# A hybrid decoder layer on one core: the retention's rotary step is moved out of the values' group

## Chip, cores and metric

The kernel runs on one core of one Trainium2 chip. The metric is the device time of one execution in microseconds (us). The profile shows five engines of that core: PE (matmuls; PEld loads its weights), DVE (vector), ACT (scalar), POOL (GpSimd) and SP, whose queue issues nearly all DMAs.

## What is computed

One decoder layer on 1024 tokens of width 2048, in fp32. A conditioned RMSNorm gives h; one projection `h @ w_in` gives 8192 columns, which are q, k, v, z of eight stick-breaking heads and q, k, v, z of eight retention heads, each of 128 columns. The part that the change touches is the retention's rotary step and the loop behind it:

```python
def rotary(t):
    ...
    t1, t2 = tf[..., :half], tf[..., half:]
    return jnp.concatenate([t1 * cos - t2 * sin, t1 * sin + t2 * cos], axis=-1)
...
qr = rotary(split_heads(q_r, RET_HEADS))
kr = rotary(split_heads(k_r, RET_HEADS)) * (HEAD_DIM ** -0.5)
vr = split_heads(v_r, RET_HEADS).astype(jnp.float32)
ob = head_group_norm(chunkwise_retention(qr, kr, vr), ret_norm_gain[layer])
ob = ob * jax.nn.silu(z_r.astype(jnp.float32))

y = jnp.concatenate([oa, ob], axis=-1).astype(x.dtype) @ w_out[layer]
x = x + (gate[:, None, :] * y).astype(x.dtype)
```

## The kernel before

**Matmuls.** Every fp32 operand is cut into a high part (ACT, line 173) and a low part (DVE, line 175), and each product is three matmuls (`mm3`, lines 186 to 188) of 128x512. The projection and the output product are each done as seven products of half-size blocks (a Strassen scheme). The retention's queries come first, in a stage of their own (tile `first`), and are kept in DRAM unrotated (`rqraw`). Then come seven **groups** of 1024 columns. The first four hold the columns of the stick-breaking heads, two heads each (indices 0 to 3 of the list `groups`), the fifth the retention's keys, the sixth its values (`ACROSS`, computed transposed, by `run_across`), and the seventh its z (`LAST`).

A group has seven **products**, named by the block of h that they use, in the order T4, B11, T2, T1, B22, B21, T3. A product has eight **entries** (four column blocks, two halves of the sum). An entry is 12 matmuls and two **steps**: `tick()` is the program's clock. So a product has 16 steps and a group 112. The weights of an entry are cut three entries ahead (`LOOK`); in the values' group entries go in pairs of four steps. The finished outputs of a group come out in its last three products: half of the first head of each pair after B22's product, the other half after B21's, both halves of the second head after T3's (function `evac`, where `final` takes a finished tile).

**What runs beside it.** Other work is written as generators that are advanced once a step, or as functions due so many steps later (`later`). PE's order is written by hand through these steps. The stick-breaking attention of the heads whose columns a group made runs in the following group: two heads each in the second to fifth group, with a tail in the first product of the next group. A vector-matrix product for the gate (`gate_steps`, tile `gr`) and sums of the output weights (`sum_steps`, tile `s`) are spread over the groups.

**The DMA queue.** SP issues the DMAs in the program's order, and a DMA that has to wait for a buffer, for its data or for an earlier write holds up all behind it. For each product the factors of h come back from DRAM, 16 loads of 256 KB (`fac`, lines 279 and 281), issued 15 to 20 steps before use. Per group there are 32 raw weight loads (lines 264 and 266). All tiles of 128x512 come from one pool of 92 slots.

**The rotary step before.** The keys' group writes its 16 finished tiles (eight heads, two halves of the sequence) to DRAM (`pr_rk`). `turn_in` starts in the values' group, as soon as the last stick-breaking head is nearly done. Every three steps it takes one tile of 128x512, key and query in turn: it loads the tile (line 1393), loads it again with its halves of 64 partitions exchanged (`sw`, lines 1395 and 1396), nine steps later makes three DVE operations (lines 1401, 1402 and 1406 for a query, whose bias is added on the way, 1404 to 1406 for a key) and two steps after that writes the result to DRAM (line 1410). So a tile costs four DMAs and three DVE operations, and there are 32 of them.

**The retention.** `ret_heads` starts six entries before the last group. Each head takes 16 steps (four gaps of `RT_GAP`): it loads keys, queries and values (lines 1432 and 1436) and a mask (`dm`, line 1455), transposes the keys on PE (line 1472, tile `ktp`), makes states (line 1480, tile `up`), scores (line 1498), masked scores on DVE (line 1503, tile `pT`) and values. The eighth head begins at the third step of the output product.

Of the kernel before, what the change touches and what calls it, by code (L numbers as in the profile page):

```python
# [17 lines left out]
P = 128  # L18
# [14 lines left out]
RT_GAP = 4  # L33
# [63 lines left out]
def layer_kernel(ctx, tc, x, c, w_ada, b_ada, norm_gain, w_in, sb_q_gain, sb_k_gain, ret_norm_gain, w_out,  # L97
# [18 lines left out]
    proj = {f"{n}{h}": dr.tile([P, S], F32, name=f"pr_{n}{h}") for n in ("q", "k", "z", "v", "rk")  # L116
# [274 lines left out]
    def evac(gi, prod, q, o):  # L391
# [595 lines left out]
    def bias_steps():  # L987
# [37 lines left out]
        nc.scalar.activation(qb[64:128, 1, 0:NZ], qb[0:64, 0, 0:NZ], AF.Copy)  # L1025

# [353 lines left out]
    def turn_in():  # L1380

        while prog.get(NH - 1, 0) < 12:
            yield 1
        for i, n in enumerate(("cos", "sin")):
            for hf in range(2):
                tables[n, hf] = t = get(f"{n}_{hf}", "att")
                nc.sync.dma_start(t, rot[i][:, halves(hf)])
        yield 2

        def one(n, h, hf):  # L1390
            src = proj[f"rk{h}"] if n == "k" else rqraw[h]
            t = get(f"r{n}_{h}_{hf}", "att")
            nc.sync.dma_start(t, src[:, halves(hf)])
            sw = get(f"sw_{n}{h}_{hf}", "att")
            nc.sync.dma_start(sw[0:64, :], src[64:128, halves(hf)])
            nc.sync.dma_start(sw[64:128, :], src[0:64, halves(hf)])
            cos, sin = tables["cos", hf], tables["sin", hf]

            def rotate():
                if n == "q":  # L1400
                    nc.vector.scalar_tensor_tensor(sw, sw, qb[:, 1, h:h + 1], sin, op0=ALU.add, op1=ALU.mult)
                    nc.vector.scalar_tensor_tensor(t, t, qb[:, 0, h:h + 1], cos, op0=ALU.add, op1=ALU.mult)
                else:
                    nc.vector.tensor_tensor(sw, sw, sin, op=ALU.mult)
                    nc.vector.tensor_tensor(t, t, cos, op=ALU.mult)
                nc.vector.tensor_tensor(t, t, sw, op=ALU.add)
                put(sw)

            def back():
                nc.sync.dma_start(turned_in[n, h][:, halves(hf)], t)  # L1410
                put(t)
                turns[0] += 1
            later(9, rotate)
            later(11, back)

        for h in range(NH):
            for n in "kq":
                for hf in range(2):
                    one(n, h, hf)
                    yield 3  # L1420
        yield 12
        put(*tables.values())

    turns = [0]

    def ret_prepare(h):
# [12 lines left out]
        def values_in(n):  # L1439
            later(n, lambda: load_v(0))  # L1440
            later(n + 1, lambda: load_v(1))
# [9 lines left out]
    def ret_attention(h, r, gap):  # L1451
# [125 lines left out]
        yield gap  # L1577
# [4 lines left out]
        yield gap  # L1582
# [3 lines left out]
        yield gap  # L1586
# [4 lines left out]
        yield gap  # L1591
# [3 lines left out]
    def ret_heads():  # L1595
        nxt, values_in = ret_prepare(0)
        while phase[0] < 6:
            yield 1
        values_in(3)
        yield 2  # L1600
        for h in range(NH):
            r = nxt
            for i, wait in enumerate(ret_attention(h, r, RT_GAP)):
# [388 lines left out]
```

## Time and profile before

| | us |
|---|---|
| median of three runs (lowest 1941.51, highest 1945.44) | 1941.53 |
| the profiled execution, by its own time | 1946.04 |
| its span in the trace | 1944.0 |
| PE busy (share of the span) | 1882.3 (97%) |
| DVE busy | 1340.7 (69%) |
| ACT busy | 816.6 (42%) |
| POOL busy | 82.1 (4%) |
| bytes moved by DMA | 557.81 MB, mean 287 GB/s |

The page gives the busy time of each engine, then the span in 40 slices of 48.6 us: a digit is the busy share in tenths, and PEclk is the clock that PE was granted. The view by windows gives the same for chosen stretches, with the DMA engines' busy share and the bytes per second. The view of waits says who waited for whom. Matmuls are pipelined, so the mean duration of one (about 390 ns) is longer than the distance between two (about 227 ns).

### The profile page before, as it was taken

The numbers are of one execution on the slowest core, as the hardware profiler recorded it, in microseconds if no ns is written. First come the engines' busy times: TensorE is split into PE (matmuls) and PEld (weight loads), VectorE is DVE, ScalarE is ACT, GpSimd is POOL, SyncE is SP. The second block draws the span as 40 slices with busy tenths as digits, with TensorE's granted clock in tenths as the row PEclk, the third lists the DMA queues.
The fourth block names the chain that finished last, engine by engine and source line by source line (L and its number), as shares of the span: only waits on it lengthen the run. The fifth ranks groups of instructions, "written<-read, shape, count | busy, mean of one in ns | idle before, by whom it ended". The sixth has DMA issues, their size and how long they took to land.

```text
span 1944.0 us, 28991 instructions
## 1 busy us (share of the span) xinstructions
PE 1882.3 (97%) x9501; PEld 1546.4 (80%) x9501; DVE 1340.7 (69%) x2601; ACT 816.6 (42%) x1543; POOL 82.1 (4%) x278
## 2 busy tenths in 40 slices
PE   8999999999999999999999999977779999999998
PEld 6777788888888888888888888755668888888887
DVE  3568775666769686867686868864664547596769
ACT  3647752234544454445444543211124446543221
POOL 0000000000010001000000000000010100000000
PEclk9999999999999999999999999988889999999999
DMA  9979999998797989797978988999976664995594
GB/s 318 364 240 314 316 356 371 364 325 293 243 311 248 316 264 332 252 319 249 351 255 286 292 319 282 297 323 322 346 266 217 225 219 147 334 370 188 169 312 164
DMA packets 417522, 557.81 MB, mean 287 GB/s; under 512 B 35166, under 2 KB 203480, under 8 KB 417372
## 3 DMA queue, kind: packets, MB, share of 16 engines
q1 hardware_dynamic: 416508, 555.57, 85.9%
q8 instruction: 75, 1.23, 0.3%
q14 instruction: 75, 0.61, 0.1%
q10 hardware_dynamic: 864, 0.40, 0.1%
HBM read 461.42 MB, written 94.41 MB: 286 GB/s over the span
## 4 chain that ended last, share of the span: by engine, by line
PE 85%; DMA 9%; DVE 3%; issue 1%; SPq 1%; ACT 0%; ACTq 0%; DVEq 0%
PE pj L186 17%; PE pj L187 17%; PE pj L188 17%; PE y L188 4%; PE y L186 4%; PE y L187 4%; PE first L186 3%; PE first L188 2%; PE first L187 2%; PE accp L607 1%; DMA sw_k<-pr_rk 1%; DMA A<-in_w_in_dram 1%; PE tp_B L1286 1%; DMA rq<-rqraw 1%; PE oT L186 1%
## 5 line engine op out<-in xcount | busy, mean ns | idle before, releaser
L173 ACT ACTIVATE wh<-A 128x512 fp32r<-128x512 f32 x392 | 247.2, 632 | 469.7 <-PE pj L187 319.3
L175 DVE TENSOR_TENSOR wl<-A,wh 128x512 fp32r<-128x512 f32 x392 | 269.4, 689 | 210.5 <-ACT wh L173 200.2
L395 ACT ACTIVATE c<-pj 128x512 f32<-128x512 f32 x112 | 66.4, 600 | 135.2 <-PE pj L188 118.5
L302 DVE TENSOR_TENSOR A<-A,A 128x512 f32<-128x512 f32 x160 | 109.8, 694 | 1.7
L398 DVE TENSOR_TENSOR c<-pj,c 128x512 f32<-128x512 f32 x112 | 74.5, 687 | 42.4 <-PE pj L188 41.8
L1250 ACT ACTIVATE om<-zp,y 128x128 f32<-128x128 f32 (+2 forms) x96 | 55.8, 581 | 107.4 <-PE zp L188 67.2
L186 PE MATMUL first<-h_hi,wh_first 128*128 128x512 f32 x224 | 95.1, 424 | 0.6 <-ACT h_hi L636 0.6
L1266 DVE TENSOR_TENSOR_SCAN om<-om 128x128 f32<-128x128 f32 (+2 forms) x96 | 93.5, 974 | 1.2
L187 PE MATMUL first<-h_lo,wh_first 128*128 128x512 f32 x224 | 88.7, 396 | 0.2 <-DVE h_lo L638 0.2
L188 PE MATMUL first<-h_hi,wl_first 128*128 128x512 f32 x224 | 88.7, 396 | 0.0
L186 PE MATMUL pj<-T4h,wh 128*128 128x512 f32 x192 | 78.7, 410 | 5.6 <-issue 3.8
L186 PE MATMUL pj<-T1h,wh 128*128 128x512 f32 x200 | 81.5, 408 | 0.0
L186 PE MATMUL pj<-B22h,wh 128*128 128x512 f32 x200 | 80.1, 401 | 0.0
L186 PE MATMUL pj<-B21h,wh 128*128 128x512 f32 x200 | 79.6, 398 | 0.0
L186 PE MATMUL pj<-B11h,wh 128*128 128x512 f32 x200 | 78.8, 394 | 0.0
L188 PE MATMUL pj<-T1h,wl 128*128 128x512 f32 x200 | 78.3, 391 | 0.0
L188 PE MATMUL pj<-B22h,wl 128*128 128x512 f32 x200 | 78.2, 391 | 0.0
L187 PE MATMUL pj<-T1l,wh 128*128 128x512 f32 x200 | 78.1, 391 | 0.0
L187 PE MATMUL pj<-B21l,wh 128*128 128x512 f32 x200 | 78.0, 390 | 0.0
L187 PE MATMUL pj<-B22l,wh 128*128 128x512 f32 x200 | 78.0, 390 | 0.0
L188 PE MATMUL pj<-B21h,wl 128*128 128x512 f32 x200 | 78.0, 390 | 0.0
L187 PE MATMUL pj<-B11l,wh 128*128 128x512 f32 x200 | 78.0, 390 | 0.0
(450 smaller groups left out, 5125.2 us busy)
## 6 DMA issues: line engine op xcount, KB each, us to landing
A<-in_w_in_dram SPq DMA_DIRECT2D x228, 256.0 KB, 5.6
ada<-in_w_ada_dram SPq DMA_DIRECT2D x120, 256.0 KB, 5.5
wB<-in_w_out_dram SPq DMA_DIRECT2D x112, 256.0 KB, 5.6
gr<-in_w_ada_dram SPq DMA_DIRECT2D x64, 256.0 KB, 5.8
T2h<-fac_T SPq DMA_DIRECT2D x56, 256.0 KB, 5.5
T2l<-fac_T SPq DMA_DIRECT2D x56, 256.0 KB, 5.5
T1h<-fac_T SPq DMA_DIRECT2D x56, 256.0 KB, 5.4
T1l<-fac_T SPq DMA_DIRECT2D x56, 256.0 KB, 5.3
```

The lines of the kernel that those rows point to most:

```text
L173: nc.scalar.activation(hi[:, 0:n], src[:, 0:n], AF.Copy)
L175: nc.vector.tensor_tensor(lo[:, 0:n], src[:, 0:n], hi[:, 0:n].bitcast(F32), op=ALU.subtract)
L186: nc.tensor.matmul(o, a_hi, b_hi, start=first, stop=False, skip_group_check=on)
L187: nc.tensor.matmul(o, a_hi, b_lo, start=False, stop=False, skip_group_check=on)
L188: nc.tensor.matmul(o, a_lo, b_hi, start=False, stop=last, skip_group_check=on)
L302: nc.vector.tensor_tensor(r[o], r[a], r[b], op=ALU.add if n == 1 else ALU.subtract)
L395: nc.scalar.activation(t, o, AF.Copy)
L398: nc.vector.tensor_tensor(dst[q, cc], o, dst[q, cc], op=ALU.add)
L607: nc.tensor.matmul(ap_[32 * g:32 * g + 32, :], silu_z[:, j, :], ada[cc, j // 2][:, (j % 2) * 256:(j % 2) * 256 + 256], start=j < 4, stop=j ...
L1250: nc.scalar.activation(om[:, :n], zp[:, :n], AF.Sigmoid, scale=y[:, 16 + i:17 + i])
L1266: nc.vector.tensor_tensor_scan(rev, rev, rev, init, op0=ALU.mult, op1=ALU.bypass)
L1286: nc.tensor.transpose(banks_[j // 2][:, c0:c0 + P], be[:, j * P:(j + 1) * P], ident)
```

## The change

The values' group and the keys' group change places: values are the fifth group, keys the sixth. `turn_in` is gone. The 16 query tiles are rotated in three lots, six tiles in the third group and five each in the fourth and fifth, one tile every four steps from step 10 of the group on; the three operations stand seven steps behind the loads, and the write one step behind those. The cos and sin tables are loaded anew for each lot, and once more for the keys. A key tile isn't written to DRAM and loaded again: one step after it is finished two DMAs copy its halves of 64 partitions crosswise into a second SBUF tile, seven steps later the three operations follow, and one step after these the write. The retention's heads go in the order 0, 2, 4, 6, 1, 3, 5, 7; the first starts when its two key tiles have been written, at step 106 of the keys' group (before: at step 3 of the last group), and a head takes 17 steps in place of 16, so that the last begins two steps earlier than before. In all, SP issues 20 DMAs fewer (2166 for 2186); PE and DVE have the same operations as before.

```diff
-RT_GAP = 4
+RT_GAPS = (4, 4, 4, 5)
+QUERY_GAP = 4
+QUERIES = {2: 6, 3: 5, 4: 5}
...
-    groups.append([(5 * GW + a * P, proj[f"rk{a}"], proj[f"rk{a + 1}"]) for a in range(0, NH, 2)])
 
     ACROSS = len(groups)
     groups.append([(6 * GW, None, None)] * 4)
+    KEYS = len(groups)
+    groups.append([(5 * GW + a * P, a, a + 1) for a in range(0, NH, 2)])
     groups.append([(7 * GW + a * P, a, a + 1) for a in range(0, NH, 2)])
...
+            if gi == KEYS:
+                sw = get(f"sw_k{to}_{hf}", "att")
+
+                def swap():
+                    nc.sync.dma_start(sw[0:64, :], t[64:128, :])
+                    nc.sync.dma_start(sw[64:128, :], t[0:64, :])
+                later(1, swap)
+                later(8, lambda: rotate("k", to, hf, t, sw))
+                return
...
-    def turn_in():
-
-        while prog.get(NH - 1, 0) < 12:
-            yield 1
...
+    def rotate(n, h, hf, t, sw):
+
+        cos, sin = tables["cos", hf], tables["sin", hf]
+        if n == "q":
+            nc.vector.scalar_tensor_tensor(sw, sw, qb[:, 1, h:h + 1], sin, op0=ALU.add, op1=ALU.mult)
+            nc.vector.scalar_tensor_tensor(t, t, qb[:, 0, h:h + 1], cos, op0=ALU.add, op1=ALU.mult)
+        else:
+            nc.vector.tensor_tensor(sw, sw, sin, op=ALU.mult)
+            nc.vector.tensor_tensor(t, t, cos, op=ALU.mult)
+        nc.vector.tensor_tensor(t, t, sw, op=ALU.add)
+        put(sw)
+
+        def back():
+            nc.sync.dma_start(turned_in[n, h][:, halves(hf)], t)
+            put(t)
+            turned.add((n, h, hf))
+        later(1, back)
...
+    def turn_queries(n):
+
+        assert bias_done
+        yield 8
+        load_tables()
         yield 2
...
+        for _ in range(n):
+            h, hf = queries.popleft()
+            t = get(f"rq_{h}_{hf}", "att")
+            nc.sync.dma_start(t, rqraw[h][:, halves(hf)])
+            sw = get(f"sw_q{h}_{hf}", "att")
+            nc.sync.dma_start(sw[0:64, :], rqraw[h][64:128, halves(hf)])
+            nc.sync.dma_start(sw[64:128, :], rqraw[h][0:64, halves(hf)])
+            later(7, lambda h=h, hf=hf, t=t, sw=sw: rotate("q", h, hf, t, sw))
+            yield QUERY_GAP
+        yield 7
         put(*tables.values())
...
         load("k", 0)
         later(1, lambda: load("q", 0))
+        later(3, lambda: load_v(0))
         later(4, lambda: load("k", 1))
         later(5, lambda: load("q", 1))
-        if h:
-            values_in(3)
-        return r, values_in
...
     def ret_heads():
-        nxt, values_in = ret_prepare(0)
-        while phase[0] < 6:
+        heads = (0, 2, 4, 6, 1, 3, 5, 7)
+        while not {("k", 0, 0), ("k", 0, 1)} <= turned:
             yield 1
-        values_in(3)
-        yield 2
-        for h in range(NH):
+        nxt = ret_prepare(0)
+        yield 7
+        for i, h in enumerate(heads):
...
-            if gi == 5:
-                start(turn_in(), 1)
+            if gi in QUERIES:
+                run_apart(turn_queries(QUERIES[gi]))
+            if gi == KEYS:
+                run_apart(for_keys())
+                start(ret_heads(), 1)
```

**The queries' lots, on SP.** This is SP's order in the second product of the third group, around the small write `krow` of the stick-breaking keys' scales and its load back `kb`. `s` are loads of output weights, `concat` is the output of a finished head. Before:

```order
L1089 DMA s_1_0_7182<-in_w_out_dram 128x512
L1089 DMA s_1_0_7183<-in_w_out_dram 128x512
L1345 DMA concat_78<-zr_1_6474 128x512
L1174 DMA krow_164<-yr_7161 8x128
L1182 DMA kb_0_7219<-krow_164 128x512
L1182 DMA kb_1_7221<-krow_164 128x512
L1185 DMA q_0_7223<-pr_q_104 128x512
L1185 DMA q_1_7224<-pr_q_104 128x512
```

And now, with a tile's three loads (`rq`, `sw_q` twice) and the writes of earlier tiles (`rot_q`):

```order
L1102 DMA s_1_0_7201<-in_w_out_dram 128x512
L1102 DMA s_1_0_7202<-in_w_out_dram 128x512
L1358 DMA concat_78<-zr_1_6466 128x512
L1187 DMA krow_156<-yr_7180 8x128
L1430 DMA rq_1_7229<-rqraw_95 128x512
L1432 DMA sw_q_1_7231<-rqraw_95 64x512
L1433 DMA sw_q_1_7231<-rqraw_95 64x512
L1408 DMA rot_q_146<-rq_1_7083 128x512
L1195 DMA kb_0_7247<-krow_156 128x512
L1195 DMA kb_1_7249<-krow_156 128x512
L1198 DMA q_0_7251<-pr_q_104 128x512
L1198 DMA q_1_7252<-pr_q_104 128x512
```

Two loads of a query tile and a write have come between `krow` and `kb`, and another four rows ahead of them.

**The end of the rotated keys, on SP.** This is where the first retention head's keys are loaded (`rk_0<-rot_k`, first head, first half). `A` are raw weights of the next group, `rv` values. Before, at the end of the values' group:

```order
L1396 DMA sw_q_1_15222<-rqraw_101 64x512
L266 DMA A_6_1_1_15235<-in_w_in_dram 128x4x128
L1432 DMA rk_0_15237<-rot_k_146 128x512
L1410 DMA rot_k_153<-rk_0_15069 128x512
L1432 DMA rq_0_15246<-rot_q_154 128x512
L1039 DMA gr_6_15267<-in_w_ada_dram 128x2x256
L279 DMA T4h_6_15271<-fac_T_6_216 128x512
L281 DMA T4l_6_15273<-fac_T_6_216 128x512
L279 DMA T4h_7_15275<-fac_T_7_217 128x512
```

And now, at steps 97 to 103 of the keys' group, where `rot_k_138` is the first head's:

```order
L416 DMA sw_k_0_15073<-c_5_3_14268 64x512
L417 DMA sw_k_0_15073<-c_5_3_14268 64x512
L269 DMA A_6_3_0_15099<-in_w_in_dram 128x4x128
L1408 DMA rot_k_138<-c_5_0_14206 128x512
L269 DMA A_6_0_1_15122<-in_w_in_dram 128x4x128
L1452 DMA rk_0_15124<-rot_k_138 128x512
L1452 DMA rq_0_15135<-rot_q_146 128x512
L1408 DMA rot_k_140<-c_5_1_14224 128x512
L269 DMA A_6_1_1_15149<-in_w_in_dram 128x4x128
L1456 DMA rv_0_15160<-rvt_0_134 128x4x128
L1452 DMA rk_1_15173<-rot_k_138 128x512
```

Before, the keys that are loaded had been written long ago (a write `rot_k` beside them is another head's); now the load stands two rows behind the write of the same tile.

**The same stretch on DVE,** at the beginning of the last group: from the cut `wl` of one entry's weights to that of the next, `ga` being the gate's sums and `A` sums of raw weights. Before:

```order
L175 TENSOR_TENSOR wl_4_3_0_15376<-A_6_3_0_14686,wh_4_3_0_15374 128x512
L1048 SCALAR_TENSOR_TENSOR ga_13330<-gr_6_15267,silu_c,ga_13330 128x256 x2
L302 TENSOR_TENSOR A_6_0_0_14601<-A_6_0_0_14601,A_6_0_0_15093 128x512
L302 TENSOR_TENSOR A_6_0_0_15093<-A_6_0_0_14844,A_6_0_0_15093 128x512
L175 TENSOR_TENSOR wl_4_0_1_15411<-A_6_0_1_14728,wh_4_0_1_15409 128x512
```

And now, with both halves of a key tile (`c` and `sw_k`, lines 1402 to 1404) in between:

```order
L177 TENSOR_TENSOR wl_4_3_0_15376<-A_6_3_0_14672,wh_4_3_0_15374 128x512
L1061 SCALAR_TENSOR_TENSOR ga_13476<-gr_6_15215,silu_c,ga_13476 128x256 x2
L305 TENSOR_TENSOR A_6_0_0_14581<-A_6_0_0_14581,A_6_0_0_15012 128x512
L1402 TENSOR_TENSOR sw_k_1_15231<-sw_k_1_15231,sin_14595 128x512
L1403 TENSOR_TENSOR c_5_0_14568<-c_5_0_14568,cos_14591 128x512
L1404 TENSOR_TENSOR c_5_0_14568<-c_5_0_14568,sw_k_1_15231 128x512
L1402 TENSOR_TENSOR sw_k_0_15233<-sw_k_0_15233,sin_14593 128x512
L1403 TENSOR_TENSOR c_5_0_13997<-c_5_0_13997,cos_14589 128x512
L1404 TENSOR_TENSOR c_5_0_13997<-c_5_0_13997,sw_k_0_15233 128x512
L305 TENSOR_TENSOR A_6_0_0_15012<-A_6_0_0_14789,A_6_0_0_15012 128x512
L177 TENSOR_TENSOR wl_4_0_1_15422<-A_6_0_1_14691,wh_4_0_1_15420 128x512
```

Six operations of a key tile pair have come between two cuts; three more such pairs follow, one between each of the next cuts.

More of the change, by code (lines that the diff above doesn't have):

```diff
@@ L115, in layer_kernel @@
     rqraw = [dr.tile([P, S], F32, name=f"rqraw{h}") for h in range(NH)]
-    proj = {f"{n}{h}": dr.tile([P, S], F32, name=f"pr_{n}{h}") for n in ("q", "k", "z", "v", "rk")
+    proj = {f"{n}{h}": dr.tile([P, S], F32, name=f"pr_{n}{h}") for n in ("q", "k", "z", "v")
             for h in range(NH)}
@@ L1387, in turn_in, with for_keys @@
                 nc.sync.dma_start(t, rot[i][:, halves(hf)])
-        yield 2
[L1390 to L1414, printed above, removed]
-        for h in range(NH):
[L1417 to L1421, printed above, removed]
-        put(*tables.values())
-    turns = [0]
+    queries = deque((h, hf) for h in range(NH) for hf in range(2))
+    def turn_queries(n):
+        assert bias_done
+        yield 8
+        load_tables()
+        yield 2
+        for _ in range(n):
[8 more added lines that the diff above has]
+        yield 7
+        put(*tables.values())
+    def for_keys():
+        yield 60
+        load_tables()
+        while len(turned) < 4 * NH:
+            yield 1
+        put(*tables.values())
     def ret_prepare(h):
@@ L1576, in ret_attention @@
         scores(0)
[L1577 removed]
+        yield RT_GAPS[0]
         turn_k(1)
@@ L1792, in layer_kernel @@
             cut_right(3 - left_over, 0)
-        if gi == ACROSS and j + 6 < len(entries) and entries[j + 6][0] != ACROSS and entries[j + 5][0] == ACROSS:
-            start(ret_heads(), 1)
         if gi != ACROSS:
```

26 lines of the change are left out of this document (14 added, 12 removed).

## The prediction

> **What bounds the kernel now.** I read the page first: which engine is busy, and where it is not.
>
> ```profile
> span 1944.0 us, 28991 instructions
> ...
> PE 1882.3 (97%) x9501; PEld 1546.4 (80%) x9501; DVE 1340.7 (69%) x2601; ACT 816.6 (42%) x1543; POOL 82.1 (4%) x278
> ...
> PE   8999999999999999999999999977779999999998
> ...
> PEclk9999999999999999999999999988889999999999
> ```
>
> PE bounds the kernel. Its only weak place is slices 27 to 30 (1264 to 1458 us), where it is seven to eight tenths busy and its clock drops too. Next comes the view by windows, cut where PE changes from one product to the next. Columns: stretch, its length, busy us of each engine, then PEclk, DMA share and GB/s.
>
> ```profile
> 229.00:403.00 174.00, 174.00 (x770) 144.06 (x769) 112.48 (x176) 64.65 (x110) 0.00 (x0) 1.00 1.04 357
> 622.00:646.00 24.00, 24.00 (x113) 19.59 (x112) 18.32 (x34) 8.60 (x16) 0.00 (x0) 1.00 0.58 192
> 646.00:672.00 26.00, 26.00 (x126) 21.50 (x125) 14.53 (x26) 12.03 (x25) 3.04 (x14) 1.00 1.03 350
> 820.40:842.50 22.10, 22.00 (x99) 17.91 (x98) 16.67 (x34) 8.30 (x15) 0.00 (x0) 1.00 0.81 276
> 1182.70:1197.00 14.30, 14.17 (x78) 12.01 (x77) 14.00 (x25) 4.04 (x8) 0.00 (x0) 1.00 0.93 326
> 1211.00:1255.30 44.30, 44.28 (x194) 36.00 (x193) 38.75 (x64) 13.02 (x22) 0.00 (x0) 1.00 0.96 299
> 1255.30:1392.50 137.20, 104.08 (x386) 79.50 (x384) 77.97 (x126) 24.90 (x42) 0.00 (x0) 0.87 1.04 326
> 1392.50:1439.80 47.30, 33.93 (x149) 28.43 (x150) 28.27 (x56) 7.85 (x13) 2.55 (x2) 0.79 0.98 330
> 1439.80:1622.80 183.00, 183.00 (x1037) 158.70 (x1037) 100.33 (x307) 88.46 (x166) 15.53 (x12) 1.00 0.65 215
> ```
>
> 1211 to 1255 are two products of the values' group, B11 and T2, with no PE stall: 22.15 us each, 1.38 us a step. The next four take 137.2 us where 4 x 22.15 = 88.6 would do: 48.6 lost. The last group's first product takes 47.3; its other six take 30.5 each with a retention head in every 16 steps (8.4 us a head), so with 13 steps of a head it should take 28.9: 18.4 lost. Together 67.0 us are at stake. Who ends the waits there:
>
> ```profile
> DVE sw_q L1401 <- DMA sw_q<-rqraw: 31.7, 12, 5.7
> PEld pj L187 <- DVE wl L175: 26.7, 11, 7.2
> DVE sw_k L1404 <- DMA sw_k<-pr_rk: 22.5, 8, 6.6
> PE pj L187 <- DVE wl L175: 21.6, 9, 6.8
> PE up L1480 <- DMA rv<-rvt: 11.6, 1, 11.6
> DVE pT L1503 <- DMA dm<-in_ret_mask_dram: 13.6, 1, 13.6
> ```
>
> PE waits for cut weights, DVE cuts them in order behind a rotation, and the rotation waits for its exchanged halves. And the transfers are late because there are too many (DMA issues of 1255.3 to 1392.5):
>
> ```profile
> DMA packets 33835, 44.68 MB, mean 326 GB/s; under 512 B 3049, under 2 KB 15648, under 8 KB 33828
> ...
> rq<-rqraw SPq DMA_DIRECT2D x11, 256.0 KB, 5.8
> sw_q<-rqraw SPq DMA_DIRECT2D x22, 128.0 KB, 6.0
> rot_k<-rk SPq DMA_DIRECT2D x11, 256.0 KB, 6.2
> rk<-pr_rk SPq DMA_DIRECT2D x10, 256.0 KB, 6.1
> sw_k<-pr_rk SPq DMA_DIRECT2D x20, 128.0 KB, 5.4
> ...
> rk<-rot_k SPq DMA_DIRECT2D x1, 256.0 KB, 6.0
> ```
>
> The view lists 190 issues in 137.2 us: 1.39 a us, with the DMA engines at 1.04 (the window's row). Between 229 and 403 they are at 1.04 too; there nearly all transfers have 256 KB (0.262 MB), and 357 GB/s are 1.36 a us. So with 42 half-size transfers among the 190 the bytes fall, the number stays, and a half lands no sooner than a whole tile (5.4 and 6.0 us against 5.8 and 6.1). I take 1.39 DMAs a us as the limit, whatever their size. The stretch held 21 rotated tiles (11 `rq`, 10 `rk`), so one cost PE 48.6 / 21 = 2.3 us.
>
> **The change part by part.** *Rotation leaves the values' group.* A product of 16 steps asks there for 16 factors, some 5 raw tiles, 2 gate tiles and 16/3 x 4 = 21 transfers of the rotation: 44, or 32 us of DMA in 22 us of PE. Without the rotation it is 23, or 17 us, and PE is late for nothing. The last group's first product lost its time to `rv`, loaded right behind the writes of the values, and to `dm`, late in the same queue; the values are now written a whole group earlier. So both losses go, 1946.0 - 67.0 = 1879.0, and what is late next is below.
>
> *Values' group fifth, beside stick-breaking heads.* Its weights are cut only four steps ahead, not six. At 1182.7 this mixture stands already, since the last heads' tail runs in the values' first product: DVE is busy 14.00 of 14.30 us and PE 14.17, without a wait of note. Cost 0; if a fuller mixture differs, it shows in C.
>
> *The queries' lots.* In the third group's second product SP's count rises from 28 to 44, in 24.0 us, in which 33 go: 11 are left, 8 us behind. What covers that? Before, B11 and T2 of the values' group asked for 82 (by SP's order) in 44.3 us, in which 62 go: 20 left, 15 us behind, and PE stood nowhere. The operations now stand seven steps behind the loads, not nine, which takes 2 x 1.38 off: 12 us of cover for 8. The next product (26.0 us, 31 asked, 36 go) pays back. SP itself waits for DVE at each `rot_q`, with the factors queued behind; those are issued 16 steps (22 us) ahead of use and take some 6, so that they can stand the 8 too. On DVE a tile is three operations at their distance in the timeline:
>
> ```profile
> 1270.29 0.68 DVE L1404 TENSOR_TENSOR sw_k<-sw_k,sin 128x512 f32<-128x512 f32 x1
> 1270.89 0.68 DVE L1405 TENSOR_TENSOR rk<-rk,cos 128x512 f32<-128x512 f32 x1
> 1271.61 0.69 DVE L1406 TENSOR_TENSOR rk<-rk,sw_k 128x512 f32<-128x512 f32 x1
> 1272.21 0.69 DVE L175 TENSOR_TENSOR wl<-A,wh 128x512 fp32r<-128x512 f32 x1
> ```
>
> That is 1.9 us, and four tiles are 8 us a product. In the third group 18.32 + 8 is 2.3 over the 24.0, in the fourth 16.67 + 8 is 2.6 over the 22.1; what is queued behind a rotation are the cuts of weights, and three entries of them stand ready (6 x 1.38 = 8.3 us). Cost 0; if the cover fails, 16 x 2.3 = 37. Below zero it can't be: nothing is taken away there, and PE has no wait to lose.
>
> *Keys rotated as they come.* Up to step 80 little is asked (9 to 19 DMAs in 8 steps). In the last 32 steps it is 91: 49 factors, raw and gate tiles, 22 exchanges, 8 writes of rotated keys, 12 loads for the first two retention heads. That takes 65 us, where PE needs 44 and some 3 for the first head's beginning: up to 18 behind. Ahead of the write of the first head's key (step 99) are 46 of them, in 19 steps: 33 us for 26, 7 behind. The load of that key waits for the write. The nearest wait of this kind is
>
> ```profile
> SPq L1182 <- DMA krow<-yr: 5.1, 4, 1.9
> ```
>
> a load behind a write of 4 KB, which SP waited out each time. Here a whole tile's write takes 6.2 (`rot_k`) and the load 6.0 (`rk<-rot_k`): 7 + 12.2 = 19.2 us behind step 99. PE wants the tile for `ktp` at step 106, 9.7 us behind step 99. So PE waits 9.5, or 2.5 if SP is level; I take 7, nearer to the upper end, because the writes of the other heads' keys, each waiting for DVE, keep SP from running ahead before it.
>
> `dm` stands 21 rows behind that load: 15 us, and 5.5 to land, so 14.5 us after the key has landed. DVE's `pT`, due one step after `ktp`, waits for it, as it did for 13.6 before. Behind `pT` stand, up to the cut for step 16 of the last group, 50 operations of 128x512 (24 of them rotations) at 0.60 us, 6 of the gate, 7 of the states and 8 of the statistics:
>
> ```profile
> L1048 DVE SCALAR_TENSOR_TENSOR ga<-gr,silu_c,ga 128x256 f32<-128x256 f32 x17 | 8.2, 482 | 0.3
> L1490 DVE SCALAR_TENSOR_TENSOR state<-state,up 128x128 f32<-128x128 f32 x6 | 1.7, 286 | 0.2
> ```
>
> 30 + 2.9 + 2.0 and some 2 for the statistics: 37 us. PE has from step 106 to there 6 x 1.38, the 3 of the head's beginning and 16 x 1.9: 41.7 us. So 14.5 + 37 - 41.7 = 10 late. Bounds: 4 if `dm` leaves sooner, 14 if the exchanges are late as well. A wait of PE also costs clock:
>
> ```profile
> 1298.88 0.80 PE L187 MATMUL pj<-wl,B22h 128*128 128x512 f32 x1 [6.78 <-DVE wl L175]
> 1299.48 0.63 PE L188 MATMUL pj<-wh,B22l 128*128 128x512 f32 x1
> 1299.90 0.63 PE L186 MATMUL pj<-wh,B22h 128*128 128x512 f32 x1
> ```
>
> matmuls 0.42 us apart, not 0.227: 1 to 2 us each time, 3 in all. Sum for this end 7 + 10 + 3 = 20.
>
> How soon an exchange inside SBUF lands, no row shows. The nearest are the halves from DRAM (5.4 and 6.0), far below them the small write (1.9 at most). I take 5.5, by the halves, which have the same shape; at 1.9 the 22 exchanges hold no place in the queue for long, and SP is level there. The Trainium skill (SBUF — State Buffer, "The DMA setup-cost knee") has a fixed cost of about 2 us and bytes over 436 GB/s: an estimate of 2.3 us for a half, and the end would cost about 11, not 20. The rows of the halves are more than twice that, so the trace doesn't agree so far.
>
> *Heads of 17 steps, nine steps earlier.* Same matmuls; the last head starts two steps sooner. 0.
>
> **Sum:** 1879.0 + 20 = 1899 on the profiled execution. That execution lay 4.5 us above the median of 1941.53, beside the slowest of the three runs (1945.44); I take off 4: 1895.
>
> **The rivals.** *A, the forecast:* 1895, own range 1882 to 1904 (end of keys 7 to 29).
>
> *B, the end of the keys is nearly free.* The limit is bytes, not number, and exchanges inside SBUF take none of HBM's: then the other 69 x 0.262 MB at 357 GB/s are 51 us for 47, SP is nearly level, the key's wait is 2.5, `dm` costs 4 and the clock 1: 1879 + 8 - 4 = 1883. Against it stand 326 GB/s with the DMA engines at 1.04; for it, that SP in that stretch also stood waiting for DVE, so that the number may have been held down by DVE and not by the queue. The Trainium skill (DMA: Bandwidth & Descriptors, "Bandwidth") says so: about 358 GB/s bind for HBM to SBUF, 435 for SBUF to SBUF. By that rule it would be B; the first stage's 357 agrees, the 326 does not.
>
> *C, the lots aren't covered.* 16 query tiles at 2.3 us: 1895 + 37 = 1932. For it: DVE was at 18.32 of 24.0 and 16.67 of 22.1 before a tile is added, and the stick-breaking heads have loads and DVE steps of their own in the same queue (`kb`, behind two query tiles now). Against it: PE's 44.28 of 44.30 with a tile every three steps.
>
> *D, slower.* A rotated tile costs PE its 2.3 us wherever it stands, since DVE waits in order for its halves: 32 x 2.3 = 74, and the first head 18.4 as before: 1879 + 92 - 4 = 1967. It decides if SP falls more than 12 us behind in each lot; I count 8.
>
> **How the numbers follow.** A 0.55, B 0.25, C 0.12, D 0.06; 0.02 for no change. A and B hold 0.8 and span 1879 to 1904; with part of C the range is 1878 to 1914. The measurement of this kernel tells 0.2% (3.9 us) from no change: faster 0.92, same 0.02, slower 0.06.
>
> **What would show it.** Right: the values' group's last four products with PE full and clock 1.00; no PE stall in the third to fifth group's second product; near the last group's start PE waiting for `ktp` on the DMA of `rk` (3 to 10 us), DVE for `dm`, and some 10 us on `wl`. Wrong: exchanges landing near 2 us and SP level (B); `sw_q` ending DVE's waits and DVE PE's in the lots (C, D).

## The result and the profile after

The changed kernel takes 1913.87 us, median of four runs (1912.11 to 1914.28); the kernel before took 1942.79 on the same chip (four runs, 1941.51 to 1945.44). The ratio is 0.9848, with a 95% interval of 0.9831 to 0.9865: 29 us faster. The forecast was 1895 with a range of 1878 to 1914: the direction was right, and the time came out at the very edge of the range's slow end. The profiled execution took 1914.28 by its own time. The page of the changed kernel:

```profile
span 1912.1 us, 28962 instructions
...
PE 1870.4 (98%) x9501; PEld 1542.4 (81%) x9501; DVE 1338.7 (70%) x2601; ACT 818.1 (43%) x1543; POOL 85.0 (4%) x278
...
PE   8999999999999999999999999999689999999998
...
PEclk9999999999999999999999999999899999999999
```

The weak place has shrunk from four slices to two and has moved to 1338 to 1434 us, where the rotated keys end and the retention heads begin. Cut where PE changes from one group to the next, the two traces compare so:

| stretch | before | after |
|---|---|---|
| third group | 197.3 | 198.0 |
| fourth group | 196.7 | 200.4 |
| fifth group (keys before, values after) | 196.4 | 197.5 |
| sixth group (values before, keys after) | 209.8 | 180.1 |
| last group | 230.3 | 222.8 |

The same view by windows inside the last three rows and at one place of the fourth group (the second product), of the changed kernel:

```profile
820.30:846.20 25.90, 23.75 (x99) 19.21 (x98) 23.33 (x44) 8.31 (x15) 0.00 (x0) 0.93 0.75 253
1187.40:1221.00 33.60, 30.28 (x149) 25.31 (x149) 28.85 (x49) 9.88 (x19) 0.00 (x0) 0.95 0.63 210
1221.00:1329.80 108.80, 108.80 (x482) 90.09 (x481) 56.91 (x94) 31.77 (x54) 0.00 (x0) 1.00 0.87 283
1329.80:1367.60 37.80, 27.18 (x130) 22.74 (x129) 15.10 (x25) 6.35 (x11) 0.00 (x0) 0.86 0.99 292
1367.60:1412.70 45.10, 35.22 (x166) 29.88 (x165) 41.48 (x83) 8.99 (x15) 4.96 (x4) 0.85 0.89 273
1412.70:1590.60 177.90, 177.90 (x991) 153.67 (x990) 99.64 (x302) 86.67 (x163) 13.03 (x11) 1.00 0.68 227
```

1221 to 1330 are five products of the keys' group, 21.8 us each with PE full. The values' group, whose last four products were slow, stands fifth now, with PE busy 195.9 of 197.3 us at a clock of 1.00 (990.1 to 1187.4): the four slow products are gone. Beside them stand three losses: the fourth group's second product (25.9 where it took 22.2 before), the first product of the sixth group (33.4 by PE's rows, 33.6 in the window above, where it took 28.5), and the two products at the keys' end, T3 (37.8) and the last group's T4 (45.1). The waits there, from the view of waits (us in total, times, longest):

```profile
DVE pT L1519 <- DMA dm<-in_ret_mask_dram: 16.4, 1, 16.4
...
PE ktp L1488 <- DMA rk<-rot_k: 9.8, 1, 9.8
...
PE tp_B L1299 <- DVE al L1324: 4.5, 4, 3.2
...
PE op L1532 <- DVE state L1506: 4.0, 1, 4.0
...
PE op L1532 <- DVE state L1504: 3.8, 1, 3.8
...
PE yp L1182 <- DVE y L162: 2.1, 1, 2.1
```

And the timeline of SP's queue at the keys' end (start, duration of the issue; the lines between are other loads):

```profile
1342.02 0.47 SPq L416 DMA_DIRECT2D sw_k<-c  x1
1342.68 0.47 SPq L417 DMA_DIRECT2D sw_k<-c  x1
...
1344.18 0.34 SPq L1408 DMA_DIRECT2D rot_k<-c  x1
1344.86 0.37 SPq L269 DMA_DIRECT2D A<-in_w_in_dram  x1
1350.12 0.34 SPq L1452 DMA_DIRECT2D rk<-rot_k  x1
...
1364.38 0.46 SPq L1471 DMA_DIRECT2D dm<-in_ret_mask_dram  x1
```

with two lines of DVE's timeline, in brackets the wait ahead of the instruction:

```profile
1348.86 0.69 DVE L1402 TENSOR_TENSOR sw_k<-sw_k,sin 128x512 f32<-128x512 f32 x1 [5.48 <-DMA sw_k<-c]
...
1370.63 0.69 DVE L1519 TENSOR_TENSOR pT<-sp,dm 128x512 f32<-128x512 f32 x1 [16.44 <-DMA dm<-in_ret_mask_dram]
```

The reader can follow the forecast chain here. The key's write leaves at 1344.18, SP issues one load more and stands until the write has landed (1350.12), and the key is there at 1353.2, where PE's wait for `ktp` ends. The mask leaves 14.3 us after the key's load and lands at 1370.6; until then DVE does nothing, with the cuts of weights behind it. The waits of PE in this stretch sum to 20.6 us, and PE's clock is 0.86 and 0.85 in the two windows.

### The profile page after: what moved, and what is told of

It is laid out like the page before. It is cut to its first block, busy times and chain, and to the rows that moved or that the text cites. A ratio compares the mean times of both kernels' runs of the same rounds, so it can differ in the third digit from the quotient of the medians.

```text
span 1912.1 us, 28962 instructions
## 1 busy us (share of the span) xinstructions
PE 1870.4 (98%) x9501; PEld 1542.4 (81%) x9501; DVE 1338.7 (70%) x2601; ACT 818.1 (43%) x1543; POOL 85.0 (4%) x278
## 4 chain that ended last, share of the span: by engine, by line
PE 85%; DMA 8%; DVE 5%; issue 1%; SPq 0%; ACT 0%; ACTq 0%; DVEq 0%
PE pj L188 18%; PE pj L189 17%; PE pj L190 17%; PE y L190 4%; PE y L189 4%; PE y L188 4%; PE first L188 3%; PE first L190 2%; PE first L189 2%; PE accp L619 1%; PE tp_B L1299 1%; PE oT L188 1%; PE oT L190 1%; PE oT L189 1%; PE zp L190 1%; PE zp L189 1%
## 5 line engine op out<-in xcount | busy, mean ns | idle before, releaser
L190 PE MATMUL pj<-B11h,wl 128*128 128x512 f32 x200 | 78.6, 393 | 0.0
```

What stands on the lines that cost most here:

```text
L190: nc.tensor.matmul(o, a_lo, b_hi, start=False, stop=last, skip_group_check=on)
```

## The experiments

All times are medians; the ratio is to the kernel before, measured beside each on the same chip. T3 and T4 are the keys' last product and the last group's first, in us, cut in the trace as above (in `e7_queries` the values' last product stands for T3).

| kernel | us | ratio (95%) | T3 | T4 |
|---|---|---|---|---|
| changed kernel | 1913.87 | 0.9848 (0.9831 to 0.9865) | 37.8 | 45.1 |
| `e1_mask` | 1904.24 | 0.9805 (0.9788 to 0.9821) | 36.4 | 38.2 |
| `e2_later` | 1918.40 | 0.9880 (0.9866 to 0.9895) | 25.6 | 57.3 |
| `e3_both` | 1907.53 | 0.9822 (0.9807 to 0.9837) | 26.8 | 45.2 |
| `e7_queries` | 1905.56 | 0.9810 (0.9796 to 0.9825) | 21.8 | 42.5 |
| `e4_quarters` | 1923.09 | 0.9896 (0.9879 to 0.9913) | 42.8 | 46.4 |
| `e5_odd` | 1907.70 | 0.9820 (0.9802 to 0.9838) | 37.6 | 37.2 |
| `e8_spread` | 1898.20 | 0.9772 (0.9753 to 0.9791) | 35.9 | 29.5 |
| `e9_spread_later` | 1896.77 | 0.9770 (0.9748 to 0.9792) | 22.5 | 38.2 |
| `e10_kept` | 1893.25 | 0.9752 (0.9734 to 0.9770) | 27.3 | 32.6 |
| `e6_noq` | 1909.04 | 0.9828 (0.9813 to 0.9842) | 36.6 | 45.3 |
| `e11_lot` | 1889.06 | 0.9731 (0.9718 to 0.9744) | 30.1 | 31.8 |
| `e12_rot` | 1885.45 | 0.9708 (0.9695 to 0.9722) | 25.4 | 30.9 |

From `e8_spread` on, the intervals of neighbours in a chain (e8, e10, e11, e12) overlap, and so do those of `e5_odd` and `e6_noq` with the changed kernel's. What such a step is worth is read from the products in its trace, one profiled execution each, and not from the time alone.

### The mask, and where the first head starts

The theory was two chains: the first key's way through DRAM, and the mask behind it. The rivals were an overfull DVE and a queue that is late as a whole. First the mask alone:

```diff
-        nc.sync.dma_start(dm, ret_mask[h])          # in ret_attention
+        nc.sync.dma_start(r["dm"][...], ret_mask[h])  # in ret_prepare, ahead of load("k", 0)
```

> Each retention head's mask tile is loaded with its first key, not when its attention starts. Theory: the 28 us that the keys' end costs are two chains, the key's round trip (ktp 9.8 us) and the mask behind it (DVE 16.4 us at pT, then op and pj). The mask then lies ready, pT waits only for the scores (sp, 1364), DVE is free some 6 us sooner, the last group's first product falls from 45.1 to 37-41 us, ktp keeps its 9 to 11 us, and the time is 1904-1910. Rival 1 (DVE is simply overfull there with 24 rotations between the cuts): DVE's wait goes, the product stays at 43-46, 1911-1915. Rival 2 (the queue is late as a whole): another transfer (rq, rv) ends the waits that dm ended, 1911-1916.

```profile
1328.50:1364.90 36.40, 27.91 (x130) 23.28 (x129) 21.16 (x37) 6.48 (x11) 2.57 (x2) 0.86 1.02 307
1364.90:1403.10 38.20, 31.88 (x166) 27.05 (x165) 35.57 (x72) 8.96 (x15) 2.61 (x2) 0.96 0.99 293
```

T4 fell by 6.9 us to 38.2, T3 kept the key's wait (8.5), and the time is 1904.24: as the theory had it. Then the first head later:

```diff
-RT_GAPS = (4, 4, 4, 5)
+RT_GAPS = (4, 4, 4, 4)
...
         nxt = ret_prepare(0)
-        yield 7
+        yield 15
```

> The first retention head starts eight steps later and the heads are 16 steps again, so that the last ends where it did. Theory: ktp's wait (9.8 us) and sp's (0.9) go, since the key lands 3 us before its new place; the mask is issued 8 steps later too and pT still waits for it, but by then DVE has done most of the rotations: the keys' last product falls from 38.0 to 25-28 us, the last group's first stays at 38-45; 1895-1904. Rival 1 (DVE overfull): the keys' last product is cured and the same loss appears on wl in the last group's first product, which grows past 50: 1908-1914. Rival 2 (queue late as a whole): ktp still waits 5 us or more.

The theory failed here. T3 was cured (25.6), T4 grew to 57.3, and the two sum to 82.9 us as in the changed kernel, though they hold fewer matmuls, since the later head's stand behind them. Here are the two products together, of the changed kernel and of this one; PE stands idle 20.5 and 27.1 us:

```profile
1329.80:1412.70 82.90, 62.40 (x294) 52.62 (x293) 56.58 (x108) 15.35 (x25) 4.96 (x4) 0.86 0.94 282
```

```profile
1328.50:1411.40 82.90, 55.81 (x246) 45.80 (x245) 52.44 (x93) 13.41 (x22) 2.93 (x2) 0.81 0.90 275
```

The view of waits of this kernel, from 1300 to 1420 us, shows who waited:

```profile
PE op L1532 <- DVE state L1504: 12.1, 1, 12.1
...
DVE pT L1519 <- DMA dm<-in_ret_mask_dram: 10.7, 1, 10.7
...
DVE ga L1061 <- DMA gr<-in_w_ada_dram: 9.7, 2, 7.8
...
PE pj L190 <- DVE wl L177: 7.9, 2, 5.5
...
PE op L1530 <- DVE pT L1519: 7.1, 1, 7.1
```

and the same view of SP's queue, from 1310 us on:

```profile
SPq L1408 <- DVE c L1404: 12.2, 5, 5.7
```

Where these waits stand in time, by the timelines of DVE and of SP's queue:

```profile
1366.30 1.01 DVE L1061 SCALAR_TENSOR_TENSOR ga<-gr,silu_c,ga 128x256 f32<-128x256 f32 x2 [7.81 <-DMA gr<-in_w_ada_dram]
...
1385.70 0.69 DVE L1519 TENSOR_TENSOR pT<-sp,dm 128x512 f32<-128x512 f32 x1 [10.71 <-DMA dm<-in_ret_mask_dram]
```

```profile
1359.81 0.98 SPq L1052 DMA_DIRECT2D gr<-in_w_ada_dram  x1
...
1380.17 0.46 SPq L1471 DMA_DIRECT2D dm<-in_ret_mask_dram  x1
```

DVE waits first for a gate tile `gr` (7.8 us, until 1366.30), then for the mask (10.7, until 1385.70). The gate tile leaves SP at 1359.81 and the mask at 1380.17; from 1349 to 1384 SP issues 52 transfers, one every 0.68 us. So both come late because many transfers stand ahead of them. SP waits for DVE too, since a rotated key is written only when DVE has rotated it, but all of these 12.2 us lie behind 1381 us, when the gate tile has landed and the mask has been issued, so they are not what delays either. With PE no longer held up at `ktp`, its `op` meets the late mask (7.1) and the rotations that are piled up behind it on DVE (12.1). The first rival had named the place, if not the size.

Both edits together:

> Both edits: the mask with the first key, the first head eight steps later. Theory: both chains are gone, what stays is DVE's 24 rotations between the cuts of the last group's first product: keys' last product 25-27 us, the next 32-38, PE clock 0.95 or better there; 1888-1896. Rival 1 (DVE overfull): the last group's first product stays at 42 or more, 1900-1908. Rival 2 (queue): no better than the later head alone within 2 us.

1907.53, T4 at 45.2: the first rival's 42 or more. The mask's part comes off the later head too (1918.40 to 1907.53), but the later head is worth nothing by itself. SP waits for DVE less than 1 us at a time here, and DVE still waits 7.8 us for the gate tile. That leaves the piled-up rotations as a third cost, apart from the key and the mask; the next kernels test it.

### The rotations on DVE

The odd heads' 24 operations on DVE are left out in one kernel (in `rotate`):

```diff
         else:
-            nc.vector.tensor_tensor(sw, sw, sin, op=ALU.mult)
-            nc.vector.tensor_tensor(t, t, cos, op=ALU.mult)
-        nc.vector.tensor_tensor(t, t, sw, op=ALU.add)
+            if h % 2 == 0:
+                nc.vector.tensor_tensor(sw, sw, sin, op=ALU.mult)
+                nc.vector.tensor_tensor(t, t, cos, op=ALU.mult)
+        if n == "q" or h % 2 == 0:
+            nc.vector.tensor_tensor(t, t, sw, op=ALU.add)
```

In another, with the early mask, each odd head's tile is exchanged and rotated four steps behind the last:

```diff
+                wait = SPREAD * (to % 2) * (2 * q + 1 - hf)     # SPREAD = 4
-                later(1, swap)
-                later(8, lambda: rotate("k", to, hf, t, sw))
+                later(1 + wait, swap)                            # which itself adds later(7, rotate)
```

> The changed kernel with the odd heads' keys not rotated: their 24 operations on DVE are left out, their exchanges, writes and loads stay, so the last four heads' part of the output is another. Theory (DVE is overfull in the last group's first product): that product falls from 45.1 to 33-38 us though the mask's wait (16.4) stays, and the keys' last product stays at 36-39; 1902-1907. Rival (the queue is late, DVE only waits for it): DVE's 14 us come back as waits for dm and sw_k or wl, 1910-1914.

> The mask with the first key, and the odd heads' keys spread: one tile's exchange and rotation every four steps, not eight in eight steps (those heads come fifth to eighth and don't need them sooner). Theory (between e1's 1904.2 and no loss stand the bunched rotations, 7 us, and the key's round trip, 8.5): the last group's first product falls from 38.2 to 31-34 us, ktp still waits 7 to 10; 1896-1900. Rival (the queue): the product stays over 36; 1901-1905.

T4 of the first (its mask still comes late: DVE waits 17.2 us for it), and T3 and T4 of the second:

```profile
1365.60:1402.80 37.20, 31.75 (x166) 27.10 (x165) 23.69 (x55) 9.01 (x15) 2.95 (x3) 0.91 0.99 305
```

```profile
1329.80:1365.70 35.90, 27.75 (x130) 23.09 (x129) 21.24 (x37) 6.39 (x11) 2.57 (x2) 0.86 1.00 306
1365.70:1395.20 29.50, 29.50 (x166) 25.54 (x165) 26.73 (x59) 8.89 (x15) 2.88 (x2) 1.00 1.02 315
```

Leaving the operations out takes 7.9 us off T4 (1907.70, just above the 1902 to 1907 expected). Spreading them, with nothing left out, makes T4 full (PE 29.50 of 29.50, clock 1.00), though the DMA engines are as busy as in `e1_mask` (1.02 and 0.99). Spreading moves the exchanges too; `e5_odd`, which keeps every transfer where it was, ties the cost to DVE. So the operations cost time because they stood in one heap between the cuts, and the queue was no bound of that product. What is left is the key's 8.2 us in T3.

> As the spread kernel, and the first head eight steps later with heads of 16 steps. Theory: with the rotations spread the later head now pays, since nothing is piled up behind it on DVE: the waits for the gate tile (7.8 us) and of op (6.7) that the later head met before are gone, ktp waits for nothing; 1888-1894, 6 to 10 below the spread kernel. Rival (the end of the keys costs what its transfers cost, wherever the head starts): within 2 us of the spread kernel or above it.

The spread kernel with the later head (`yield 15`, gaps of 4) takes 1896.77 against 1898.20: equal within the intervals, as the rival had it. T3 falls to 22.5, T4 rises to 38.2, where DVE waits 7.5 us for the gate tile; part of the shift is the head's own work, which moves from T3 to later products, and PE stands idle 8.1 us of the two products in either kernel. (Its profiled execution took 1903.31, 6.5 above the median.) Starting the head later again only moves the loss.

### Number or bytes

```diff
-                    nc.sync.dma_start(sw[0:64, :], t[64:128, :])
-                    nc.sync.dma_start(sw[64:128, :], t[0:64, :])
+                    for i in range(0, P, 32):
+                        j = (i + 64) % P
+                        nc.sync.dma_start(sw[i:i + 32, :], t[j:j + 32, :])
```

> The changed kernel with each exchange of halves as four transfers of 32 partitions, not two of 64: same bytes, 22 transfers more in the last 32 steps of the keys' group. Theory (the queue takes some 1.4 transfers a us whatever their size): 22 / 1.4 = 16 us more in the queue, 10 of them ahead of the first head's key; ktp's wait grows from 9.8 to 15-20 us and the time to 1919-1926. Rival (bytes set the pace, exchanges inside SBUF are nearly free): nothing moves, 1911-1916.

The same stretch of 45 us, of the changed kernel and of this one, and this one's wait for the key:

```profile
1300.00:1345.00 45.00, 43.41 (x192) 35.62 (x190) 28.14 (x46) 12.63 (x21) 0.00 (x0) 1.00 0.98 288
```

```profile
1300.00:1345.00 45.00, 42.71 (x189) 35.03 (x187) 28.04 (x46) 11.92 (x20) 0.00 (x0) 1.00 0.81 249
```

```profile
PE ktp L1489 <- DMA rk<-rot_k: 14.9, 1, 14.9
```

Same bytes, more transfers: 9.2 us slower and 5.1 us more for the key. The view of DMA issues has 61 transfers in the 45 us (1.36 a us), and 69 in the other kernel (1.53 a us), while the rate fell from 288 to 249 GB/s and the DMA engines to 0.81. So the number weighs, and bytes don't set the pace here: rival B falls. Not whatever the size, though: transfers of 64 KB pass somewhat faster, and `ktp` waits 14.9 us, just under the 15 to 20 expected. In this kernel SP spends 2.4 to 3.3 us on the four issues of an exchange, one behind the other, while the DMA engines are not full; the pace may be that of SP's issuing. No run took issuing and moving apart.

### One part alone

The queries' lots put into the kernel before, which keeps its keys through DRAM and its order of groups:

```diff
+            if gi in QUERIES:
+                run_apart(turn_queries(QUERIES[gi]))
...
-            for n in "kq":
-                for hf in range(2):
-                    one(n, h, hf)
+            for hf in range(2):
+                one("k", h, hf)
```

> The kernel before with one part alone: the queries rotated in three lots in the third to fifth group; keys still through DRAM in the values' group, which stays sixth. Theory (a limit on transfers in the values' group): its 16 key tiles, one every three steps from its first product on, end in the third of its products; the four products that took 137.2 us take 92-105, the lots cost 4-8 us as in the changed kernel, the first head's waits for rv and dm (11.6 and 13.6) stay: 1903-1915, so nearly all of the gain is the queries'. Rival (a rotated tile costs PE 2.3 us wherever it stands): 16 tiles less there, 16 more in the lots, 1935-1945.

```profile
1187.90:1216.40 28.50, 28.37 (x149) 24.04 (x148) 25.31 (x43) 9.12 (x17) 0.00 (x0) 1.00 1.00 323
...
1261.10:1291.10 30.00, 25.39 (x97) 20.08 (x98) 21.28 (x36) 5.48 (x9) 0.00 (x0) 0.89 1.04 345
...
1357.60:1400.10 42.50, 30.70 (x150) 26.22 (x149) 23.43 (x49) 8.55 (x15) 2.54 (x2) 0.84 0.96 326
```

1905.56, as the theory had it: below the changed kernel, and the intervals of the two ratios don't meet. The lots alone give 36.5 us; the rest of the change, keys inside SBUF and the new order of groups, costs 7 to 8 as it stands. The keys' tiles still slow one product here (30.0), the first head still waits 11.8 us for `rv`, and the sixth group's first product has its 28.5 us, not 33.4.

### The queries' lots

DVE's timeline in the fourth group's second product, of the changed kernel: the third step of the reciprocal square root of the keys' scales (lines 160 to 162), for which PE waits at `yp`, stands behind a query tile.

```profile
822.59 0.18 DVE L162 SCALAR_TENSOR_TENSOR y<-u,y 128x16 f32<-128x16 f32 x1
...
823.89 0.74 DVE L1399 SCALAR_TENSOR_TENSOR sw_q<-sw_q,qb,sin 128x512 f32<-128x512 f32 x1
824.55 0.74 DVE L1400 SCALAR_TENSOR_TENSOR rq<-rq,qb,cos 128x512 f32<-128x512 f32 x1
825.33 0.69 DVE L1404 TENSOR_TENSOR rq<-rq,sw_q 128x512 f32<-128x512 f32 x1
825.94 0.17 DVE L160 TENSOR_TENSOR u<-y 128x16 f32<-128x16 f32 x1
```

> The changed kernel with the three DVE operations of each query tile left out; loads, exchanges and writes stay, so the rotated heads' queries go in raw and that part of the output is another. Theory (the lots' small stalls come from DVE, where the scale chain of the stick-breaking keys stands behind rotations): the fourth group's second product falls from 24.3-26.0 to 22.3 us, the third lot's product from 25.2 to 24-25; the keys' first product stays at 33 and the end of the keys as it is; 1908-1912. Rival (the lots cost nothing or their transfers do): the product stays at 24 or more, 1912-1916.

Without the three operations (`rotate` leaves them out for queries) the product takes 22.3 us and the kernel 1909.04, as the theory had it. The transfers cost nothing to be seen there, though three loads of a query tile (not two, as the section on the change counts) and a write stand between `krow` and `kb`. The last two kernels get the same without leaving anything out, by moving the lots two steps; they stand on one that first takes the key's way through DRAM away:

```diff
+        if n == "k" and h == 0:
+            kept[hf] = t             # used as the first head's rk: no write, no load
```

> As the spread kernel, and the first head's key stays in SBUF after its rotation (no write, no load back), while that head's mask, queries and values are loaded from step 84 on, ahead of the crowd. Theory (what is left at the keys' end is the write and load of the first key, in a full queue): ktp's wait of 8.2 us goes and its clock with it, the keys' last product falls from 36.1 to 26-29 us (an early head's matmuls included), the last group's first product stays at 30-33; 1885-1890. Rival (another transfer is late next: sw_k for the second half, or factors): the product stays over 32 us, 1893-1898.

1893.25, not the 1885 to 1890 expected but the rival's 1893 to 1898. T3 falls from 35.9 to 27.3 us and `ktp` waits no more, as in the theory; T4 is 32.6, and DVE still waits 11.0 us in four places for exchanged halves, which the rival had named. The key kept and the earlier loads of that head's mask, queries and values were not taken apart.

```diff
         assert bias_done
-        yield 8
+        yield 10
```

> As the kernel with the first key kept, and the queries' lots start two steps later in their groups, so that no rotation stands between two steps of the stick-breaking keys' scale chain on DVE (826.46: PE waited 2.15 us for y behind a query tile's three operations). Theory: that wait goes, the fourth group's second product falls from 26.0 to 22-23 us and the rest stays; 1888-1891. Rival (any place of a lot costs the same, another chain meets it): 1892-1895.

```profile
819.80:842.00 22.20, 22.10 (x99) 18.03 (x98) 21.47 (x41) 8.52 (x15) 0.00 (x0) 1.00 0.78 248
```

1889.06, as expected, with PE full in that product although DVE is busy 21.47 of 22.20 us, a larger share than the 23.33 of 25.90 in the changed kernel (one tile's three operations have moved out of the product). So it was a tile's place among the steps of the chain that cost PE time, and not a full DVE. T3 is 30.1 in this profile, whose execution took 1891.55, where `e10_kept` had 27.3.

```diff
-                    later(7, lambda: rotate("k", to, hf, t, sw))
+                    later(10, lambda: rotate("k", to, hf, t, sw))
...
         nxt["k", 0], nxt["k", 1] = kept[0], kept[1]
-        yield 8
+        yield 5
```

> As the lot kernel, and the keys' rotations stand ten steps behind their exchanges, not seven, with the first head where it was. Theory (DVE still waits 11 us in four places for exchanged halves with cuts of weights behind it, of which PE sees 1.7 at wl and 1.5 at op): DVE's wait for sw_k falls under 4 us and the keys' last product from 27.5 to 25-26.5; 1885-1889, 1 to 4 below the lot kernel. Rival (the later rotation pushes the first head's scores, or falls into the crowded product): equal within 1 us, or above it.

```profile
1327.10:1352.50 25.40, 25.40 (x130) 21.49 (x129) 16.74 (x26) 6.44 (x11) 2.96 (x2) 1.00 1.12 315
1352.50:1383.40 30.90, 29.93 (x166) 25.62 (x165) 28.97 (x66) 8.84 (x15) 2.50 (x2) 1.00 1.05 329
```

```profile
DVE sw_k L1405 <- DMA sw_k<-c: 0.2, 1, 0.2
```

1885.45, as expected, 0.9708 of the kernel before (0.9695 to 0.9722) and 28 us below the changed kernel: the fastest of all. T3 is full, T4 lacks 1 us, and DVE's wait for exchanged halves is 0.2 us.

## Why the prediction was right, and where it fell short

**What the change takes away: right.** The 48.6 and 18.4 us lost in the values' group and behind it were put down to the rotation's transfers. With the queries' half of them gone 36.5 us came back (`e7_queries`), and with the keys' gone too the values' group runs all but full (195.9 of 197.3 us). The limit on transfers, chosen over bytes, held in the main (`e4_quarters`), though not "whatever their size".

**The end of the keys: the mechanism right in the main, the size 20 where it was 27.** Against the 56.3 us that T3 and T4 take in `e12_rot`, the changed kernel's 82.9 are 26.6 too long: 10.7 for the first key and its queries (forecast 7, bounds 2.5 to 9.5, so just past the upper one), 9.9 at `op` and `wl` behind the mask and the rotations (forecast 10), and the remaining 6.0 are put down to the clock (forecast 3): as many matmuls (294) keep PE busy 62.4 us here and 55.3 there.

The way of the first key met its sum by luck. The write left 10.4 us behind step 99 (forecast 7; PE begins T3, step 96, at 1329.65, so step 99 is 1333.8), it took 5.9 (6.2), and the load took 3.1 (6.0): 19.4 for the forecast's 19.2, with two errors that cancel. The 7 us of waiting stood below that sum's own 9.5, to leave room for an SP that is level; it was not. The reason given for that, SP waiting for DVE at other heads' keys, is not what happened: from 1310 us to the key's load all of SP's waits for DVE come to about 1 us. The mask landed 17.4 us behind the key (14.5).

The forecast put its 10 us on `wl`, and only 1.1 came there. PE met the late DVE sooner, at `op`: 4.8 us behind the mask, which are gone in `e1_mask`, and 4.0 behind the rotations, which are gone from that product in `e5_odd`. The experiments took the two products down step by step: the mask 8.3 (82.9 to 74.6), the spread rotations 9.2 (to 65.4), the key kept 5.5 (to 59.9), the later rotation 3.6 (to 56.3; 5.6 from the 61.9 of `e11_lot`, on which it stands). The forecast says nothing of a later first head. It gained nothing, since gate tile, mask and rotations then stood in the same full queue and on the same DVE.

**The step that failed: "Cost 0" for the lots and for the values' group beside the stick-breaking heads.** By the products' times they cost 10.4 us: 0.7, 3.7 and 1.1 in the third to fifth group and 4.9 in the sixth group's first product. The working asked whether SP falls behind and whether the cuts of weights are late, and for PE both stayed covered (it waits for `wl` once in the whole run, 1.1 us in the last group); it did not ask which short DVE chain with PE at its end a rotation would split. In the fourth group three operations of 0.7 us between two steps of that chain cost 2.1 us of waiting and some of clock, and `e6_noq` and `e11_lot` take just that away. The other terms are not taken apart. C and D, which had the lots dear through late transfers, are wrong by their mechanism: `e6_noq` keeps the transfers and loses the cost.

**The range: met by luck.** 1913.87 is 0.13 us inside the range of 1878 to 1914, and outside the 1882 to 1904 that the forecast gave its own mechanism, A. The upper part of the range was there for a piece of C, and what C describes is not what happened.

**The 4 us taken off for the median** were not there: the profiled execution of the changed kernel stands 0.4 above its median.

In sum 1895 + 6.6 + 10.4 + 3.6 = 1915.6, against 1913.87; the keys' five products, 21.8 us each where 22.15 was taken, make up the rest.

**Open.** The 4.9 us at the start of the sixth group are tied to the new order of groups, since `e7_queries`, with the old one, has 28.5 us there; but that kernel undoes the keys' part too. PE waits 3.2 us there for `al` in the last heads' tail; on DVE four sums of the values' last product (2.5 us from 1189.48 on) stand ahead of it that the kernel before does not have at that place. The wait is 3.2 us in `e6_noq` too, so the lots' operations are not its cause, and it is still there in `e12_rot`. No run took that apart.

## What to carry to other kernels

Work moved out of a crowded stage should be followed to the short chains of the engine that takes it, and checked for what it splits there: its sum of busy time tells little. Where a consumer stands at the end of a full queue and a full engine, shorten what stands ahead of it (keep a tile on chip, load a mask early, spread what is not due) before trying to start it later. And when a sum comes out right, compare its terms one by one: two of them may be wrong. Test the parts alone, too: here one half of the change gave more than the whole.

## What the hardware showed

An exchange of halves inside SBUF landed no sooner than the loads from DRAM in the kernel before (5.8 and 6.1 us): issued at 1342.02 and 1342.68, used at 1348.86 by a DVE that had waited for it, 6.2 us. The Trainium skill (SBUF — State Buffer, "The DMA setup-cost knee") would give an estimate of 2.3 us; the measurement decides, for a queue that is full. The Trainium skill (SBUF — State Buffer, "Door 1: The DMA port swizzle (why [64,N] ≈ [32,N])") says that 64 partitions reach half of the ports, and 32 as many. That a half takes as long as a whole tile fits that, though a full queue alone may do it. Two quarters were not as cheap as one half all the same: cutting the exchanges so cost 9.2 us in all.

The load of the first key, issued after SP had stood for 4.8 us, was there 3.1 us later, where such a load took 6.0 in the full queue before. And with 20.6 us of PE's waits scattered over two products its clock fell to 0.86: 294 matmuls kept it busy 62.4 us, and 55.3 at a clock of 1.00 in `e12_rot`.
